# Layer norms between stages: for every second inner tile ScalarE adds the shift in a pass of its own and GpSimd makes the low half

## The chip, the cores and the metric

The kernel runs on one core of one Trainium2 chip. The metric is the device time of the program in microseconds (us). Five engines with a queue each work side by side: TensorE (PE in the profile; its weight loads are listed as PEld), VectorE (DVE), ScalarE (ACT), GpSimd (POOL) and SyncE (SP), which only starts DMAs here. An engine takes its instructions in the order in which they stand in its queue, and waits at the head of the queue for what an instruction needs.

## The reference, cut to what matters

Two layers of a diffusion backbone on 512 latent tokens and 256 context tokens, width 1024. Each layer has two modulated norms, one ahead of the token mixers and one ahead of the SwiGLU feed-forward:

```
h  = _rmsnorm(x, g_norm1) * (1.0 + sc1) + sh1      # ahead of the input projection
...
x  = x + ga1 * (o @ w_out)
h2 = _rmsnorm(x, g_norm2) * (1.0 + sc2) + sh2      # ahead of the feed-forward
x  = x + ga2 * ((silu(h2 @ w_ff1) * (h2 @ w_ff3)) @ w_ff2)
```

The context stream goes through the same formulas with its own shift and scale; the second layer needs it only in its mixers. The result is the latent stream.

## The kernel before

Activations lie transposed: features on the 128 partitions, in eight inner tiles (k = 0 to 7, `KT = 8`), tokens along the free axis. All large products are made from split numbers: a weight and an activation are each held as a high half of reduced width (`F32R`) and a low half, value minus high half, and `mm3` (L237 to L241) adds three products: high by high, high weight by low activation, low weight by high activation.

`norm_apply` (L320 to L333) makes the split activation of a norm. `parts` are stretches of tokens: 0 to 512 and 512 to 768 in the first two places below, 0 to 256 and 256 to 512 in the third. For each part and each inner tile k:

- L329, VectorE: `xn = x * gsc * pb`. `gsc` is gain times (1 + scale), a column; `pb`, in PSUM, is the inverse root mean square spread over the partitions.
- L331, ScalarE: `h[0] = xn + shift`, written at reduced width: the high half.
- L332, VectorE: `h[1] = (xn + shift) - h[0]`: the low half.

`xn` is a tile of a pool with two buffers, so a third multiplication waits until a buffer is read out. `issue_after(lows[-ahead].ins)` with `ahead = 2` also puts the multiplication of a tile behind the low half of the tile two before it, in VectorE's queue.

`norm_apply` is called four times. The first call, ahead of the first layer's mixers, works `in_place`. The other three are the places that matter here, called places 1, 2 and 3: in `dense` of layer 0 (`h2`, some 486 to 510 us), in `run` ahead of the second layer's mixers (some 1076 to 1102 us), and in `dense` of layer 1 (some 1388 to 1405 us). That makes 3 x 2 x 8 = 48 tiles.

TensorE consumes the halves at once: in `dense` for the first feed-forward tile (`f == 0`), in `proj_t` for the first two projection tiles. In both it walks k from 0 to 7 for a part, six matmuls for each k (two weights, three products), and then does the next part. `norm_finish` ends a part's statistics: a chain of tiny VectorE instructions (`rsqrt`, L249 to L255) and the spreading of the result by transposes on TensorE (`bcast`, L276). The transposes of the second part stand in TensorE's queue among or behind the matmuls of the first.

Beside this, `weights` (L222 to L235) loads a 512 KB weight tile, makes its high half on ScalarE (L231) and its low half on VectorE (L232, two inputs in SBUF). The order of each queue is worked out when the program is built, by a planner that plays the program through with its own costs and takes the ready instruction of highest priority; `issue_after` and the pools bind it.

Of the kernel before, what the change touches and what calls it, by code (L numbers as in the profile page):

```python
# [12 lines left out]
AF = mybir.ActivationFunctionType  # L13
ALU = mybir.AluOpType
# [169 lines left out]
class _Core:  # L184
# [135 lines left out]
    def norm_apply(self, x, pbs, parts, gsc, sh, h, in_place=False, ks=range(KT)):  # L320
        nc = self.nc
        lows = []
        ahead = 3 if in_place else 2
        for pb, (sl, i) in zip(pbs, parts):
            w = sl.stop - sl.start
            for k in ks:
                xn = x[:, k, sl] if in_place else self.xn.tile([P, NT], F32, name="xn")[:, :w]
                with self.tc.issue_after(lows[-ahead].ins) if len(lows) >= ahead else ExitStack():
                    nc.vector.scalar_tensor_tensor(xn, x[:, k, sl], gsc[:, k, i:i + 1], pb[:, :w],  # L329
                                                   op0=ALU.mult, op1=ALU.mult)  # L330
                nc.scalar.activation(h[0][:, k, sl], xn, AF.Identity, bias=sh[:, k, i:i + 1])  # L331
                lows.append(nc.vector.scalar_tensor_tensor(h[1][:, k, sl], xn, sh[:, k, i:i + 1], h[0][:, k, sl],  # L332
                                                           op0=ALU.add, op1=ALU.subtract))  # L333
        return lows[-1]

    def setup(self):
# [1121 lines left out]
```

## Time and profile before

| | |
|---|---|
| time of three runs, median | 1770.11 us (1770.05 to 1770.53) |
| time of the profiled execution | 1768.27 us |
| its span in the trace | 1766.5 us |
| mean granted TensorE clock | 0.981 of full |
| busy share: PE, DVE, ACT, POOL | 96%, 58%, 30%, 4% |

The span is the time from the first to the last instruction in the trace; the time of the execution is 1.77 us more. The runs' median stands 1.84 us above the profiled execution. A busy TensorE is not TensorE at its peak, since matmuls overlap. "Idle before, releaser" in a row says how long the engine did nothing just before an instruction, and what ended that.

### The profile page before, as it was taken

The numbers are of one execution on the slowest core, as the hardware profiler recorded it, in microseconds if no ns is written. First come the engines' busy times: TensorE is split into PE (matmuls) and PEld (weight loads), VectorE is DVE, ScalarE is ACT, GpSimd is POOL, SyncE is SP. The second block draws the span as 40 slices with busy tenths as digits, with TensorE's granted clock in tenths as the row PEclk, the third lists the DMA queues.
The fourth block names the chain that finished last, engine by engine and source line by source line (L and its number), as shares of the span: only waits on it lengthen the run. The fifth ranks groups of instructions, "written<-read, shape, count | busy, mean of one in ns | idle before, by whom it ended". The sixth has DMA issues, their size and how long they took to land.

```text
span 1766.5 us, 25597 instructions
## 1 busy us (share of the span) xinstructions
PE 1691.6 (96%) x10142; PEld 1373.8 (78%) x10142; DVE 1017.0 (58%) x2503; ACT 528.3 (30%) x852; POOL 67.3 (4%) x116
## 2 busy tenths in 40 slices
PE   4899899999999999999999998999999999999999
PEld 1678777676878888888888886788777888888887
DVE  7887546583387545445967537376677634333443
ACT  2422344452241212121121224225444423213221
POOL 2111000000000000000000000010000000000000
PEclk9899999999999999999999999999999999999999
DMA  9245440515134435243253332342330123223232
GB/s 365 86 149 179 144 173 26 175 53 195 60 133 135 137 128 162 89 155 125 73 163 89 103 107 94 128 126 79 115 108 25 52 92 120 96 72 119 95 90 78
DMA packets 83065, 207.25 MB, mean 117 GB/s; under 512 B 15360, under 2 KB 35968, under 8 KB 82816
## 3 DMA queue, kind: packets, MB, share of 16 engines
q1 hardware_dynamic: 54160, 160.44, 27.7%
q0 software_dynamic: 7824, 29.38, 5.0%
q10 hardware_dynamic: 20960, 15.78, 2.9%
q8 instruction: 80, 1.31, 0.3%
q14 instruction: 41, 0.34, 0.1%
HBM read 185.68 MB, written 21.99 MB: 118 GB/s over the span
## 4 chain that ended last, share of the span: by engine, by line
PE 88%; DVE 6%; DMA 2%; issue 2%; ACT 1%; SPq 0%; POOL 0%; DVEq 0%; ACTq 0%
PE psD L241 63%; PE psS L932 3%; PE psD L703 3%; PE psT L703 2%; PE psQ L979 2%; PE psQ L990 1%; PE psT L241 1%; PE psQ L1045 1%; DVE lo L232 1%; PE psT L278 1%; PE psT L376 1%; PE psT L856 1%; PE psT L265 1%; PE psS L801 1%; PE psQ L1030 1%
## 5 line engine op out<-in xcount | busy, mean ns | idle before, releaser
L241 PE MATMUL psD<-big,hi 128*128 128x512 f32 (+1 forms) x2368 | 601.5, 358 | 11.4 <-ACT big L331 7.7
L241 PEld LDWEIGHTS psD<-big,hi 128*128 128x128 f32 x2368 | 395.3, 189 | 87.7 <-ACT big L331 10.4
L231 ACT CAST hi<-raw 128x1024 fp32r<-128x1024 f32 (+1 forms) x178 | 184.3, 1039 | 753.1 <-PE psD L241 653.8
L241 PE MATMUL psD<-big,lo 128*128 128x512 f32 (+1 forms) x1184 | 365.3, 356 | 0.0
L232 DVE TENSOR_TENSOR lo<-raw,hi 128x1024 fp32r<-128x1024 f32 (+1 forms) x178 | 214.6, 1210 | 175.9 <-ACT hi L231 174.1
L241 PEld LDWEIGHTS psD<-big,lo 128*128 128x128 f32 x1184 | 201.1, 189 | 35.5 <-issue 0.4
L241 PE MATMUL psD<-gh,hi 128*128 128x512 f32 (+1 forms) x528 | 163.4, 360 | 7.5 <-DVE xb L1253 7.5
L241 PE MATMUL psD<-gl,hi 128*128 128x512 f32 (+1 forms) x528 | 165.8, 359 | 0.0
L241 PE MATMUL psD<-gh,lo 128*128 128x512 f32 (+1 forms) x528 | 165.2, 358 | 0.0
L1337 DVE TENSOR_TENSOR sg<-sg,psD 128x768 f32<-128x768 f32 (+1 forms) x44 | 36.1, 820 | 151.7 <-PE psD L241 151.7
L1253 DVE SCALAR_TENSOR_TENSOR xb<-psD,mod,xb 128x512 f32<-128x512 f32 (+1 forms) x112 | 64.6, 613 | 102.0 <-PE psD L241 101.7
L241 PEld LDWEIGHTS psD<-gh,hi 128*128 128x128 f32 x528 | 89.7, 189 | 27.0 <-DVE xb L1253 11.2
L241 PEld LDWEIGHTS psD<-gl,hi 128*128 128x128 f32 x528 | 89.7, 189 | 16.5 <-issue 0.6
L241 PEld LDWEIGHTS psD<-gh,lo 128*128 128x128 f32 x528 | 89.7, 189 | 15.8
L407 DVE CUSTOM_DVE_ANT_0 junk<-wmt,cb,pcol 128x1024 f32<-128x1024 f32 x64 | 82.1, 1283 | 29.9 <-DMA wmt<-in_wmodT 28.2
L1253 DVE SCALAR_TENSOR_TENSOR xq<-psD,mod,xq 128x512 f32<-128x512 f32 (+1 forms) x64 | 42.2, 681 | 75.0 <-PE psD L241 75.0
L241 PE MATMUL psD<-h,hi 128*128 128x512 f32 (+1 forms) x288 | 75.3, 350 | 1.5 <-DVE h L332 0.9
L932 PE MATMUL psS<-k,q 64*128 64x256 f32 (+1 forms) x432 | 71.4, 325 | 1.0 <-ACT pe L1025 0.6
L932 PEld LDWEIGHTS psS<-k,q 64*128 64x128 f32 x432 | 52.2, 185 | 19.9 <-issue 9.5
L241 PEld LDWEIGHTS psD<-h,hi 128*128 128x128 f32 x288 | 50.1, 192 | 11.2 <-issue 2.7
L241 PE MATMUL psD<-on,hi 128*128 128x256 f32 (+1 forms) x176 | 51.6, 332 | 1.2 <-ACT on L1081 1.1
L241 PE MATMUL psD<-on,lo 128*128 128x256 f32 (+1 forms) x176 | 50.2, 324 | 0.0
(404 smaller groups left out, 2321.3 us busy)
## 6 DMA issues: line engine op xcount, KB each, us to landing
raw<-in_w_ff SPq DMA_DIRECT2D x132, 512.0 KB, 3.6
wmt<-in_wmodT SPq DMA_DIRECT2D x48, 512.0 KB, 4.0
wm<-in_wmod SPq DMA_DIRECT2D x28, 512.0 KB, 6.4
raw<-in_winT SPq DMA_DIRECT2D x18, 512.0 KB, 4.2
room<-in_wmod SPq DMA_DIRECT2D x12, 512.0 KB, 11.8
nab<-in_nab SPq DMA_DIRECT2D x8, 640.0 KB, 5.2
rot<-trot POOLq DMA_DIRECT2D x8, 576.0 KB, 6.1
cf<-in_four POOLq DMA_DIRECT2D x8, 520.0 KB, 5.3
```

The source lines that it names most:

```text
L231: nc.scalar.copy(hi, raw)
L232: nc.vector.tensor_sub(lo, raw, hi)
L241: nc.tensor.matmul(o, lhsT=lhs[i], rhs=rhs[j][..., s], start=start and n == 0, stop=stop and n == 2)
L265: nc.tensor.matmul(pc[:, t], lhsT=s[:rows, t * P:(t + 1) * P], rhs=sel, start=True, stop=True)
L278: self.nc.tensor.matmul(dst, lhsT=src, rhs=self.ident, start=True, stop=True)
L376: nc.tensor.matmul(ps[32 * j:32 * j + 32], lhsT=self.cvec[:, k], rhs=ws[k // 2][:, k % 2], start=half == 0, stop=half == 1)
L407: nc.vector.tensor_tensor_reduce(junk, w, cb[:, i], 1.0, self.pcol[1][:, PC_B + f:PC_B + f + 1], op0=ALU.mult, op1=ALU.add, accum_out=mod[ ...
L703: nc.tensor.matmul(ps, lhsT=h[i][:, k, tk], rhs=w[j][:, k % per], start=k == 0 and q == 0, stop=k == KT - 1 and q == 2)
L932: self.nc.tensor.matmul(dst, lhsT=q2[i][h, qc], rhs=view(k2[j][h]), start=n == 0, stop=n == 2)
L979: nc.tensor.transpose(pp[:, k - k0], pe[:, k * P:(k + 1) * P], self.ident)
L1253: self.nc.vector.scalar_tensor_tensor(x[:, m, sl], ps[:, sl], gate[:, m, i:i + 1], x[:, m, sl], op0=ALU.mult, op1=ALU.add)
L1337: nc.vector.tensor_mul(sg, sg, pp[1])
```

## The change

Tiles with an even k, and all tiles of the in-place call, stay as they were. For odd k the shift is added by a pass of its own on ScalarE, in place in the float32 tile; a second ScalarE pass copies it to the high half; and GpSimd subtracts to make the low half. The list `lows` then holds only the low halves of even tiles, so `lows[-2]` reaches four tiles back where it reached two.

```
-                nc.scalar.activation(h[0][:, k, sl], xn, AF.Identity, bias=sh[:, k, i:i + 1])
-                lows.append(nc.vector.scalar_tensor_tensor(h[1][:, k, sl], xn, sh[:, k, i:i + 1], h[0][:, k, sl],
-                                                           op0=ALU.add, op1=ALU.subtract))
+                if in_place or k % 2 == 0:
+                    nc.scalar.activation(h[0][:, k, sl], xn, AF.Identity, bias=sh[:, k, i:i + 1])
+                    lows.append(nc.vector.scalar_tensor_tensor(h[1][:, k, sl], xn, sh[:, k, i:i + 1], h[0][:, k, sl],
+                                                               op0=ALU.add, op1=ALU.subtract))
+                else:
+                    nc.scalar.activation(xn, xn, AF.Identity, bias=sh[:, k, i:i + 1])
+                    nc.scalar.copy(h[0][:, k, sl], xn)
+                    nc.gpsimd.tensor_sub(h[1][:, k, sl], xn, h[0][:, k, sl])
```

## Rows read from the trace of the kernel before

**Rows 1.** The page, part 1: busy us (share of the span) and instructions.

```profile
PE 1691.6 (96%) x10142; PEld 1373.8 (78%) x10142; DVE 1017.0 (58%) x2503; ACT 528.3 (30%) x852; POOL 67.3 (4%) x116
```

**Rows 2.** Groups by line and shape, VectorE: busy us, mean ns, idle before.

```profile
L332 DVE SCALAR_TENSOR_TENSOR big<-xn,mod,big 128x256 fp32r<-128x256 f32 x32 | 14.3, 482 | 2.2 <-ACT big L331 2.2
L332 DVE SCALAR_TENSOR_TENSOR big<-xn,mod,big 128x512 fp32r<-128x512 f32 x16 | 11.6, 747 | 0.0
L329 DVE SCALAR_TENSOR_TENSOR xn<-xb,gsc,psQ 128x512 f32<-128x512 f32 x16 | 11.5, 742 | 0.0
...
L329 DVE SCALAR_TENSOR_TENSOR xn<-xb,gsc,psQ 128x256 f32<-128x256 f32 x16 | 6.9, 476 | 4.5 <-PE psQ L276 4.5
```

**Rows 3.** The same view, ScalarE.

```profile
L331 ACT ACTIVATE big<-xn,mod 128x256 fp32r<-128x256 f32 x32 | 14.7, 503 | 23.1 <-DVE xn L329 23.1
...
L331 ACT ACTIVATE big<-xn,mod 128x512 fp32r<-128x512 f32 x16 | 11.3, 723 | 12.2 <-DVE xn L329 12.2
```

**Rows 4.** Stretches: us, then PE, PEld, DVE, ACT, POOL busy (count), granted clock, DMA share, GB/s.

```profile
486.19:501.04 14.85, 13.52 (x58) 10.68 (x53) 12.25 (x31) 5.72 (x8) 0.00 (x0) 0.89 0.38 155
488.00:492.50 4.50, 4.50 (x16) 3.62 (x16) 4.50 (x11) 1.79 (x3) 0.00 (x0) 0.62 0.83 341
501.46:510.07 8.61, 7.46 (x48) 6.19 (x48) 6.76 (x16) 3.95 (x9) 0.00 (x0) 1.00 0.00 0
1076.43:1092.60 16.17, 14.05 (x52) 10.18 (x53) 14.71 (x33) 7.55 (x10) 0.00 (x0) 0.89 0.38 131
1388.38:1397.60 9.22, 8.15 (x54) 7.98 (x54) 8.27 (x33) 3.82 (x8) 0.00 (x0) 0.81 0.33 113
```

**Rows 5.** Timeline, place 1, VectorE: start, us, instruction, idle before.

```profile
501.46 0.87 DVE L329 SCALAR_TENSOR_TENSOR xn<-xb,gsc,psQ 128x256 f32<-128x256 f32 x2 [2.95 <-PE psQ L276]
502.51 0.89 DVE L332 SCALAR_TENSOR_TENSOR big<-xn,mod,big 128x256 fp32r<-128x256 f32 x2 [0.18 <-ACT big L331]
503.32 0.87 DVE L329 SCALAR_TENSOR_TENSOR xn<-xb,gsc,psQ 128x256 f32<-128x256 f32 x2
```

**Rows 6.** Timeline, place 1, TensorE.

```profile
498.24 0.86 PE L241 MATMUL psD<-big,hi 128*128 128x512 f32 x3
...
499.64 0.86 PE L241 MATMUL psD<-big,hi 128*128 128x512 f32 x3
...
502.54 0.91 PE L241 MATMUL psD<-big,hi 128*128 128x256 f32 x3 [1.11 <-ACT big L331]
```

**Rows 7.** Timeline, place 2, weight loads that waited for a low half.

```profile
1087.24 0.19 PEld L241 LDWEIGHTS psD<-big,hi 128*128 128x128 f32 x1 [0.42 <-DVE big L332]
...
1090.18 0.19 PEld L241 LDWEIGHTS psD<-big,hi 128*128 128x128 f32 x1 [0.31 <-DVE big L332]
```

**Rows 8.** Timeline, place 3, TensorE at the end of the first part.

```profile
1396.78 0.38 PE L276 MATMUL psQ<-cst,nr 128*128 128x128 f32 x2
```

**Rows 9.** Timeline, GpSimd: four copies, and a DMA issue behind place 2.

```profile
18.78 0.82 POOL L668 COPY ro<-sm 128x768 f32<-128x768 f32 x1 [12.06 <-DVE sm L517]
...
37.47 3.46 POOL L594 COPY bd<-bd 128x128 f32<-128x128 f32 x1
...
78.21 0.33 POOL L594 COPY bd<-bd 128x128 f32<-128x128 f32 x1 [5.15 <-DVE bg L586]
...
885.92 0.51 POOL L668 COPY ro<-sm 128x384 f32<-128x384 f32 x1 [17.72 <-DMA trot<-ro]
...
1100.19 0.54 POOL L711 DMA_DIRECT2D wglu<-in_wglu  x1 [87.61 <-DVE big L332]
```

**Rows 10.** Timeline, VectorE beside the first two of those copies.

```profile
18.38 0.20 DVE L491 SCALAR_TENSOR_TENSOR sm<-sm,sm 128x48 f32<-128x48 f32 x1
...
18.62 1.03 DVE L491 SCALAR_TENSOR_TENSOR sm<-sm,sm 128x48 f32<-128x48 f32 x2
...
40.10 0.67 DVE L632 TENSOR_TENSOR gt<-sm,bg 128x512 f32<-128x512 f32 x1
```

## Prediction

> **What bounds the kernel now.** I read the page first: TensorE is busy for 96% of the span and VectorE for 58% [rows 1]. So an engine other than TensorE matters only where TensorE waits for it. The change touches 24 of the 48 tiles of places 1, 2 and 3, so I went to the groups of L329, L331 and L332 for the price of each pass [rows 2, 3], then to the stretches and timelines of the three places to see who waits for whom.
>
> The prices: a multiplication takes 0.48 us on 256 columns and 0.74 on 512, a ScalarE pass 0.50 and 0.72, a low half 0.48 and 0.75 [rows 2, 3]. A handover costs about 0.035 us: at 501.46 a multiplication starts, 0.48 and 0.50 later would be 502.44, and the low half starts at 502.51, two handovers later [rows 5].
>
> TensorE needs 1.40 us for an inner tile of 512 columns at the full clock (498.24 to 499.64, six matmuls, 0.23 each [rows 6]), and half of that, 0.70, for 256 columns. VectorE has four passes for a pair of tiles, 2 x 0.74 + 2 x 0.75 = 2.98 us at 512 columns against TensorE's 2.80. At 256 columns its pairs come every 1.86 us (501.46 to 503.32 [rows 5]) against TensorE's 1.40. So:
>
> - Places 1 and 2, second part (256 columns): VectorE's and ScalarE's alternation sets the pace.
> - Place 2, first part (512): VectorE is busy 14.71 of 16.17 us, TensorE is busy 14.05 [rows 4] and waits 0.42 and 0.31 us for low halves [rows 7]. VectorE sets the pace here too.
> - Place 1, first part: TensorE lost time at a granted clock of 0.62 (488 to 492.5 us [rows 4]), is behind from then on, and does not wait. The low half of the last tile is wanted by the third matmul of the inner tile that starts at 499.64, so at 500.1.
> - Place 3, first part: again a mean clock of 0.81 [rows 4] and TensorE behind; it is in the last inner tile at 1396.8 [rows 8].
>
> A relief of VectorE could therefore pay in places 1 and 2. Whether this one does depends on the length of the new path.
>
> **The change, part by part.** VectorE loses 24 low halves: 8 x 0.75 + 16 x 0.48 = 13.7 us. ScalarE gains 24 passes, 8 x 0.72 + 16 x 0.50 = 13.8 us (the copy taken at the price of the pass with shift, as both read and write the same tile shape). That is covered: per pair ScalarE then has 3 x 0.50 = 1.5 or 3 x 0.72 = 2.2 us, less than any pace found below, and it is busy for 5.72 of 14.85 us and 3.95 of 8.61 us now [rows 4]. GpSimd gains 24 subtractions. The looser `issue_after` is priced at nothing, since the two buffers of `xn` bind first; without that cover it could only start multiplications earlier.
>
> The trace shows no subtraction on GpSimd. The nearest rows are copies with one input: 0.51 us for 384 columns and 0.82 for 768 [rows 9], so 0.34 us for 256 and 0.55 for 512. That is the lower bound, since a subtraction reads two inputs. The upper bound is the copy that took 3.46 us for 128 columns [rows 9], although the same shape took 0.33 at 78.21. I take twice the undisturbed copy, for two inputs: 0.65 and, rounded up from 1.10, 1.15 us. The Trainium skill, "GPSIMD Engine Reference", section 3, gives 4497 ns for a subtraction's sister, an add, on 2048 float32 columns; an estimate from that is 0.56 and 1.12 us, and by it the sum below would be about 1.3 us less.
>
> Why 3.46 us? The copy at 37.47 ends at 40.93, and VectorE's run of instructions with two inputs in SBUF ends at 40.77 [rows 9, 10]: GpSimd got through only when they were done. It works the other way as well: two instructions at 18.62 on VectorE took 1.03 us where the one at 18.38 took 0.20, beside a GpSimd copy from 18.78 to 19.60. I read this as an exclusion. The low halves (L332) and L232 have two inputs in SBUF; the multiplication (L329) reads only one there and should run free. So a low half of an even tile and the subtraction of an odd one shut each other out, and I add half a subtraction per pair: 0.33 us (256) and 0.58 us (512). The Trainium skill, "SBUF — State Buffer", section "Who interferes with whom", says just this: a VectorE instruction with two SBUF inputs contends with a GpSimd instruction that reads SBUF, and the later one blocks until the first is through; the rows agree in both directions. By that rule the sum is the one below, without it the second rival's.
>
> Now the pace. An `xn` buffer is held from the multiplication until the tile is read out. At 256 columns:
>
> - even tile: 0.48 + 0.50 + 0.48 and three handovers = 1.56 us
> - odd tile: 0.48 + 0.50 + 0.50 + 0.65 and four handovers = 2.27 us
>
> Two buffers serve two tiles per pair, so a pair takes at least (1.56 + 2.27) / 2 = 1.92 us, with the exclusion 2.25, against 1.86 now. The first odd low half comes at 0.39 + 2.24 = 2.63 us (the second multiplication of 0.87 for two starts 0.39 after the first) where it came at 502.51 + 0.89 - 501.46 = 1.94. One 256-column part thus loses 0.69 + 3 x 0.39 = 1.9 us, where TensorE has nothing else to do.
>
> At 512 columns the even tile holds 2.31 us, the odd one 0.74 + 0.72 + 0.72 + 1.15 + 0.14 = 3.47; a pair takes 2.89 us at least, 3.47 with the exclusion. The odd low halves come at 4.1 (0.7 + 3.44) and then every 3.47: the last 14.5 us after the start.
>
> - Place 1, first part: 486.19 + 14.5 = 500.7, wanted at 500.1: +0.6. Second part: +1.9.
> - Place 2, first part: the second pair waits for weights anyway; two pairs follow at 3.47 where VectorE had 2.98: +1.0. Second part: +1.9.
> - Place 3, first part: 1388.38 + 2.63 + 3 x 2.25 = 1397.8, wanted at 1396.8: +1.0. Second part: nothing; there TensorE has the matmuls of the next feed-forward tile to put in between. Without that cover it would lose up to 1.9 as well.
>
> What is given back: TensorE now stands idle 1.11 us ahead of place 1's second part, because the transposes (L276) stand behind all matmuls of the first part [rows 6]. If the planner sees TensorE wait for a last low half, it puts the transposes ahead of that, as it does at place 3 already [rows 8]. I credit half of it, 0.55, in places 1 and 2 (between 0 and 1.11).
>
> GpSimd's queue: the subtractions stand ahead of the DMA issues of `s5` (L711 and on), which already wait for the last low half until 1100.19 [rows 9]. They move with it by some 3 us and serve the stage behind the projections, so nothing. VectorE's queue: a multiplication of an odd tile that waits for GpSimd holds up the low half of the next even tile, and TensorE waits for that; this is inside the pace above.
>
> Sum: place 1 0.6 + 1.9 - 0.55 = 1.95; place 2 1.0 + 1.9 - 0.55 = 2.35; place 3 1.0; together **+5.3 us**. On the profiled execution's own 1768.27 us (its span and 1.77 us around it) that is 1773.6; on the median of the runs, 1770.11, which stands 1.84 us above it, 1775.4.
>
> The bounds: with subtractions of 0.34 and 0.55 us and no exclusion, a pair takes 1.76 us at 256 columns and TensorE's 2.80 at 512. A 256-column part loses 0.4 and wins 3 x 0.1, place 2's first part wins 2 x 0.18, and the idle 1.11 us come back twice: 0.1 - 1.11 + 0.1 - 0.36 - 1.11 = -2.4, so 1767.7. With 3.46 us for each subtraction a 256-column pair takes 3.32, the first odd low half comes at 5.4, and the three places lose 12.5, 10 and 7: 1800.
>
> **The rivals.**
>
> - *Faster.* VectorE is relieved of 13.7 us and GpSimd keeps up. Place 2's first part, where TensorE stands idle 16.17 - 14.05 = 2.1 us [rows 4], gets all of that back; with the 2 x 1.11 us, and 0.1 lost in each of the two 256-column parts, that is -4.1 or 1766.0. It decides where an odd tile's path is no slower than the pace of now: a subtraction under 0.54 us at 256 columns ((1.56 + 1.62 + 0.54) / 2 = 1.86) and under 0.97 at 512, without exclusion. For it: the lower bound. Against it: two inputs, and the exclusion of [rows 9, 10].
> - *Hidden.* My subtraction, but the exclusion costs nothing because the instructions fall between each other: pairs of 1.92 and 2.89 us. A 256-column part loses 0.69 + 3 x 0.06 = 0.87, place 2's first part wins 0.2, place 3 loses nothing, the transposes give back 0.55 to 1.11 each: +0.4 to -0.7, so 1770 to 1771.
> - *The clock falls.* With pairs of 2.25 us TensorE works 1.40 of them and waits 0.85, where it now waits 0.46 and keeps a granted clock of 1.00 [rows 4]. After the light stretch ahead of place 1 it was granted 0.62 (a mix of its two levels, 1.2 and 2.4 GHz) for 4.5 us, a loss of 0.38 x 4.5 = 1.7. If it falls in a 256-column part, a pair costs 2.80 instead of 2.25, 2.2 us more for four, and 1.7 behind it: 3.9 us in each of two places, so 1783.
>
> **How the numbers follow.** A measurement of this kernel can tell about 0.2%, 3.5 us, from no change. The forecast (+3.5 to +9 us) gets 0.50, since it rests on an exclusion that two rows show; hidden 0.27; the clock, or GpSimd held up far longer, 0.13; faster 0.10. So faster 0.10, within 0.2% 0.27, slower 0.63. The range leaves out most of the faster case and the top of the clock case: 1768 to 1786. The planner's new order moves instructions beyond these places too; that is in the range, not in the sum.
>
> **What would show it.** In the changed profile: 24 subtractions near 0.65 and 1.15 us, some stretched where they meet L332 or L232; VectorE busy down by about 13 us and ScalarE up by as much; multiplications of odd tiles that wait for POOL; pairs of about 2.25 us in the 256-column parts of places 1 and 2; TensorE's waits there put down to POOL; L276 ahead of the last matmuls of the first part. I am wrong if the subtractions take 0.5 us or less, if the pairs stay at 1.9, if the clock falls behind these waits, or if the difference arises away from the three places.

## The result and the profile after

The changed kernel takes 1779.23 us (median of 12 runs, 1774.32 to 1783.36) where the kernel before, run beside it, takes 1770.08 (12 runs): +9.2 us, a ratio of 1.0053 with a 95% interval of 1.0037 to 1.007. It is slower by 0.5%, as forecast, and inside the range; the forecast was +5.3. The profiled execution took 1774.55 us with a span of 1772.8. Behind L331 all line numbers of the changed kernel are shifted: L332 and L333 are an even tile's pass and low half, L336, L337 and L338 an odd tile's added shift, copy and subtraction; `s5`'s DMA issues are L716 and on.

The busy line of the page, against [rows 1]:

```profile
PE 1696.6 (96%) x10142; PEld 1377.0 (78%) x10142; DVE 1011.8 (57%) x2479; ACT 539.8 (30%) x876; POOL 90.0 (5%) x140
```

ScalarE gained 11.5 us, but VectorE lost only 5.2 of the forecast 13.7. The groups by line and shape say what the passes cost, against [rows 2, 3] (us in all, mean ns, idle before):

```profile
L338 POOL TENSOR_TENSOR big<-xn,big 128x256 fp32r<-128x256 f32 x16 | 11.8, 736 | 145.7 <-DMA raw<-in_w_ff 126.0 <-ACT big L337 19.7
L338 POOL TENSOR_TENSOR big<-xn,big 128x512 fp32r<-128x512 f32 x8 | 10.9, 1360 | 91.2 <-ACT big L337 91.2
L336 ACT ACTIVATE xn<-xn,mod 128x256 f32<-128x256 f32 x16 | 8.2, 509 | 12.4 <-DVE xn L329 8.9 <-POOL big L338 3.4
L333 DVE SCALAR_TENSOR_TENSOR big<-xn,mod,big 128x256 fp32r<-128x256 f32 x16 | 7.9, 496 | 6.0 <-ACT big L332 6.0
...
L333 DVE SCALAR_TENSOR_TENSOR big<-xn,mod,big 128x512 fp32r<-128x512 f32 x8 | 6.5, 809 | 2.0 <-ACT big L332 2.0
...
L337 ACT CAST big<-xn 128x256 fp32r<-128x256 f32 x16 | 6.4, 399 | 0.3
...
L337 ACT CAST big<-xn 128x512 fp32r<-128x512 f32 x8 | 4.9, 611 | 0.1
```

The subtraction takes 0.74 and 1.36 us, the copy only 0.40 and 0.61; the low halves grew by 0.01 and 0.06. Now the stretches: place 1 and the 6 us behind it, place 2 and the 8.4 us behind it (us, busy by engine, granted clock, DMA share, GB/s). A place runs here from its first multiplication to the end of its last matmul on the normed tile.

```profile
482.21:508.09 25.88, 22.57 (x107) 17.51 (x102) 17.73 (x39) 13.53 (x25) 8.11 (x8) 0.87 0.23 91
508.09:514.09 6.00, 4.51 (x17) 3.89 (x18) 4.53 (x5) 5.02 (x5) 0.00 (x0) 0.72 0.40 114
1077.12:1108.05 30.93, 22.59 (x102) 16.93 (x102) 20.06 (x41) 15.71 (x27) 12.43 (x16) 0.89 0.32 103
1108.05:1116.45 8.40, 7.00 (x21) 5.58 (x21) 2.45 (x2) 2.99 (x4) 0.00 (x0) 0.61 0.91 353
```

By the same ends the kernel before has 23.88 us in place 1 (486.19 to 510.07) and 25.21 in place 2 (1076.43 to 1101.64), and behind them granted clocks of 1.00 and 0.80. So place 1 costs 2.0 us more, place 2 costs 5.7 more, and TensorE comes out of both at a lower clock, a mix of its two levels, 1.2 and 2.4 GHz. From the first multiplication of place 3 to the end of the span it is 0.4 us more (1394.31 to 1772.80, 378.49 us, for 1388.38 to 1766.50, 378.12). The stretch between places 1 and 2 is 2.7 us longer: 1.5 of it lies right behind place 1, and 1.3 at a clock of 0.98 for 1.00 around 725 to 831 us, where the change does nothing. The stretch between places 2 and 3 is 0.5 shorter, and the one ahead of place 1, which the change does not touch, was 4.0 us shorter. Together 2.0 + 2.7 + 5.7 - 0.5 + 0.4 - 4.0 = 6.3 us, the difference of the two spans.

Where place 2's 5.7 us go is seen on the timelines of its end (start, us, idle before): GpSimd, then the ScalarE copy and the TensorE wait that answer to it.

```profile
1101.35 0.73 POOL L338 TENSOR_TENSOR big<-xn,big 128x256 fp32r<-128x256 f32 x1 [1.99 <-ACT big L337]
1102.65 0.55 POOL L716 DMA_DIRECT2D wglu<-in_wglu  x1 [0.57 <-POOL big L338]
1103.20 0.53 POOL L739 DMA_DIRECT2D rr<-tr  x1
...
1105.87 0.56 POOL L794 DMA_DIRECT2D oo<-to  x1
1106.45 0.73 POOL L338 TENSOR_TENSOR big<-xn,big 128x256 fp32r<-128x256 f32 x1
...
1102.64 0.41 ACT L337 CAST big<-xn 128x256 fp32r<-128x256 f32 x1
...
1107.23 0.39 PE L241 MATMUL psD<-big,hi 128*128 128x256 f32 x1 [3.40 <-POOL big L338]
```

The last tile's copy was done at 1103.05. Its subtraction started at 1106.45, since six DMA issues of `s5`, 0.53 to 0.77 us each, and two memsets stand ahead of it in GpSimd's queue. TensorE waited 3.40 us, more than half of what place 2 lost.

The rest of the loss is found when each place is split where TensorE begins its second part. In place 1 that is at 500.55 us, and at 502.54 in the kernel before [rows 6]. TensorE's timeline in the changed kernel, place 1:

```profile
491.80 0.43 PE L276 MATMUL psQ<-cst,nr 128*128 128x128 f32 x2
...
499.52 0.50 PE L241 MATMUL psD<-big,hi 128*128 128x512 f32 x1 [0.62 <-POOL big L338]
...
500.55 0.40 PE L241 MATMUL psD<-big,hi 128*128 128x256 f32 x2
```

The first part, of 512 columns, takes 18.34 us from the place's first multiplication (482.21 to 500.55) where it took 16.35 (486.19 to 502.54). The second part takes 7.54 us where it took 7.53. So the 2.0 us of place 1 stand in its first part alone. Place 2 is alike: its first part takes 19.98 us (1077.12 to 1097.10) for 17.68 (1076.43 to 1094.11), and its second 10.95 for 7.53, of which 3.40 are the wait for the last subtraction.

In the first part the odd tiles set the pace. Timelines of place 1, GpSimd's, ScalarE's and then VectorE's:

```profile
485.10 1.27 POOL L338 TENSOR_TENSOR big<-xn,big 128x512 fp32r<-128x512 f32 x1 [4.96 <-ACT big L337]
490.38 1.34 POOL L338 TENSOR_TENSOR big<-xn,big 128x512 fp32r<-128x512 f32 x1 [4.01 <-ACT big L337]
493.95 1.28 POOL L338 TENSOR_TENSOR big<-xn,big 128x512 fp32r<-128x512 f32 x1 [2.22 <-ACT big L337]
498.18 1.28 POOL L338 TENSOR_TENSOR big<-xn,big 128x512 fp32r<-128x512 f32 x1 [2.96 <-ACT big L337]
499.75 0.74 POOL L338 TENSOR_TENSOR big<-xn,big 128x256 fp32r<-128x256 f32 x1 [0.29 <-ACT big L337]
502.06 0.74 POOL L338 TENSOR_TENSOR big<-xn,big 128x256 fp32r<-128x256 f32 x1 [1.58 <-ACT big L337]
...
506.57 0.73 POOL L338 TENSOR_TENSOR big<-xn,big 128x256 fp32r<-128x256 f32 x1 [1.05 <-ACT big L337]
...
489.07 0.72 ACT L332 ACTIVATE big<-xn,mod 128x512 fp32r<-128x512 f32 x1
489.70 0.61 ACT L337 CAST big<-xn 128x512 fp32r<-128x512 f32 x1
...
497.10 0.49 ACT L332 ACTIVATE big<-xn,mod 128x256 fp32r<-128x256 f32 x1
...
486.90 0.75 DVE L333 SCALAR_TENSOR_TENSOR big<-xn,mod,big 128x512 fp32r<-128x512 f32 x1
487.57 0.74 DVE L329 SCALAR_TENSOR_TENSOR xn<-xb,gsc,psQ 128x512 f32<-128x512 f32 x1
...
490.50 1.25 DVE L255 SCALAR_TENSOR_TENSOR nr<-rst,nr 128x2 f32<-128x2 f32 x1
...
500.52 0.48 DVE L329 SCALAR_TENSOR_TENSOR xn<-xb,gsc,psQ 128x256 f32<-128x256 f32 x1 [0.55 <-POOL big L338]
500.92 0.48 DVE L333 SCALAR_TENSOR_TENSOR big<-xn,mod,big 128x256 fp32r<-128x256 f32 x1
501.43 0.48 DVE L329 SCALAR_TENSOR_TENSOR xn<-xb,gsc,psQ 128x256 f32<-128x256 f32 x1
```

The four subtractions of 512 columns start within 498.18 - 485.10 = 13.08 us, so a pair takes 4.36 on average, where the prediction had 3.47. The longest step shows why. The subtraction of 485.10 frees its buffer at 486.37, but the next odd tile's multiplication comes at 487.57, behind tiny instructions and an even tile's low half (486.90) in VectorE's queue; and that odd tile's copy (489.70) stands behind an even tile's pass (489.07) in ScalarE's queue. The last odd low half of the part is done at 499.46, and TensorE starts on it at 499.52.

In the second part, four subtractions of 256 columns start within 506.57 - 499.75 = 6.82 us, so a pair takes 2.27 on average, where it took 1.86 [rows 5]. That costs TensorE nothing more than before, since the tiles come earlier: the planner has put the transposes into the middle of the first part (491.80, behind all of it in the kernel before), and ScalarE makes the first high half of 256 columns at 497.10. The multiplication at 500.52 waits for the buffer that the subtraction of 499.75 holds until 500.49. The low half behind it in VectorE's queue had its input at about 500.5 but starts at 500.92, and so the next multiplication starts at 501.43.

### The profile page after: what moved, and what is told of

It is laid out like the page before. It is cut to its first block, busy times and chain, and to the rows that moved or that the text cites. A ratio compares the mean times of both kernels' runs of the same rounds, so it can differ in the third digit from the quotient of the medians.

```text
span 1772.8 us, 25645 instructions
## 1 busy us (share of the span) xinstructions
PE 1696.6 (96%) x10142; PEld 1377.0 (78%) x10142; DVE 1011.8 (57%) x2479; ACT 539.8 (30%) x876; POOL 90.0 (5%) x140
## 4 chain that ended last, share of the span: by engine, by line
PE 86%; DVE 8%; issue 2%; ACT 2%; DMA 2%; POOL 0%; SPq 0%; DVEq 0%; ACTq 0%; POOLq 0%
PE psD L241 62%; PE psS L937 4%; PE psD L708 3%; PE psT L708 2%; PE psQ L984 1%; PE psT L241 1%; PE psT L381 1%; PE psQ L995 1%; DVE lo L232 1%; PE psQ L1050 1%; PE psT L278 1%; PE psT L861 1%; PE psT L265 1%; PE psQ L1035 1%; PE psS L806 1%
## 5 line engine op out<-in xcount | busy, mean ns | idle before, releaser
L241 PE MATMUL psD<-h,lo 128*128 128x512 f32 (+1 forms) x144 | 50.4, 350 | 0.0
## 6 DMA issues: line engine op xcount, KB each, us to landing
room<-in_wmod SPq DMA_DIRECT2D x12, 512.0 KB, 11.5
```

The costliest lines, as they stand in the source:

```text
L241: nc.tensor.matmul(o, lhsT=lhs[i], rhs=rhs[j][..., s], start=start and n == 0, stop=stop and n == 2)
```

## The experiments

Three theories were on record. **Q**: the place of the last subtraction in GpSimd's queue costs place 2 its 3.4 us. **B**: in the 256-column parts the odd tile's long hold on one of two `xn` buffers sets the pace. **X**, the rival of B and the prediction's own reading: VectorE's low halves and GpSimd's subtractions shut each other out, and that sets it. Both B and X were written for the 256-column parts. All results in one table, in us; the stretch to place 3 runs from the end of place 2 to the first multiplication of place 3, the clock is the mean of the runs' granted clocks (99 runs of before, 12 of each other). The median of before is that of the 12 runs beside the changed kernel. A ratio goes by runs of before taken beside that kernel, so it is not the quotient of these medians.

| kernel | place 1 | place 2 | to place 3 | median | ratio, 95% interval | clock |
|---|---|---|---|---|---|---|
| before | 23.88 | 25.21 | 286.7 | 1770.08 | | 0.9783 |
| changed | 25.88 | 30.93 | 286.3 | 1779.23 | 1.0053 [1.0037, 1.007] | 0.9768 |
| e1_dma_behind | 25.89 | 27.73 | 286.0 | 1776.29 | 1.0037 [1.0016, 1.0058] | 0.9764 |
| e2_more_buffers | 23.70 | 28.69 | 288.7 | 1779.79 | 1.0047 [1.0026, 1.0067] | 0.9767 |
| e3_vector_subtracts | 25.00 | 25.70 | 284.2 | 1772.77 | 1.0009 [0.999, 1.0029] | 0.9781 |
| e4_before_buffers | 24.37 | 24.15 | 289.5 | 1775.86 | 1.0029 [1.0012, 1.0046] | 0.9786 |
| e6_halves | 24.25 | 29.53 | 291.8 | 1781.31 | 1.0046 [1.0024, 1.0067] | 0.9751 |
| e7_halves_dma | 24.27 | 26.14 | 284.1 | 1771.90 | 0.999 [0.9972, 1.0008] | 0.9785 |
| e8_before_halves | 24.37 | 24.28 | 293.9 | 1776.63 | 1.0017 [0.9997, 1.0038] | 0.9776 |
| e9_vector_halves | 23.09 | 23.73 | 289.8 | 1771.22 | 0.9989 [0.9968, 1.001] | 0.9791 |
| e10_vector_early | 23.08 | 23.85 | 285.2 | 1766.57 | 0.9977 [0.9952, 1.0003] | 0.9792 |
| e11_before_early | 23.05 | 24.13 | 286.7 | 1769.92 | 0.9994 [0.9974, 1.0014] | 0.9800 |
| e12_not_place2 | 25.91 | 25.14 | 288.8 | 1775.30 | 1.0032 [1.0007, 1.0057] | 0.9770 |

Place 1 by its two parts, with TensorE's granted clock in the first; each row is one profiled execution:

| kernel | first part, 512 columns | its clock | second part, 256 columns |
|---|---|---|---|
| before | 16.35 | 0.90 | 7.53 |
| changed | 18.34 | 0.81 | 7.54 |
| e12, place 1 as in the changed kernel | 18.39 | 0.91 | 7.52 |
| e8, first part as before | 17.66 | 0.81 | 6.71 |
| e11, first part as before | 16.35 | 0.90 | 6.70 |
| e2 | 16.73 | 0.80 | 6.97 |
| e3 | 16.39 | 0.79 | 8.61 |
| e7 | 18.36 | 0.91 | 5.91 |

In the changed kernel the first part takes the same time at either clock, so its length is that of the odd tiles' path. In the kernel before it depends on the clock: 16.35 us at 0.90 and 17.66 at 0.81. So the change costs the first part 2.0 us against an execution of before like the profiled one, and 0.7 against one like e8.

**e1, the queue.** In layer 1 the DMA issues are held behind the last subtraction.

```diff
-                    nc.gpsimd.tensor_sub(h[1][:, k, sl], xn, h[0][:, k, sl])
+                    self.last_sub = nc.gpsimd.tensor_sub(h[1][:, k, sl], xn, h[0][:, k, sl])
...
-            self.s5(l, oS, nq, sp, "S")
+            with tc.issue_after(self.last_sub.ins) if l == 1 else ExitStack():
+                self.s5(l, oS, nq, sp, "S")
```

> The changed kernel, with the instructions that the s5 stage of layer 1 puts into GpSimd's queue (DMA issues and memsets) held behind the last subtraction of place 2. Theory Q (the DMA issues ahead of the last subtraction made it late): the subtraction follows its ScalarE copy within 0.1 us, TensorE's wait of 3.40 us at the end of place 2 is gone, and place 2, from its first multiplication to its last matmul, takes about 27.4 us instead of 30.85 (25.21 before the change); the clock stays at full behind it, 0.7 us more. The time falls by 3.5 to 4.5 us against the changed kernel and stays about 5 us above the kernel before. Rival (the last subtraction is late by the odd tile's own path): place 2 stays at 30 us or more. Places 1 and 3 as in the changed kernel, 25.9 us and the end 374.7 us behind the first multiplication of place 3.

GpSimd's timeline at the end of place 2 in this kernel:

```profile
1111.83 0.74 POOL L338 TENSOR_TENSOR big<-xn,big 128x256 fp32r<-128x256 f32 x1 [1.99 <-ACT big L337]
1113.61 0.73 POOL L338 TENSOR_TENSOR big<-xn,big 128x256 fp32r<-128x256 f32 x1 [1.05 <-ACT big L337]
1114.80 0.55 POOL L716 DMA_DIRECT2D wglu<-in_wglu  x1 [0.45 <-PE psD L241]
```

The subtraction comes first, and place 2 falls by 3.2 us to 27.73, 2.5 above before; its second part takes 7.56 us, as before. The clock in the 8.4 us behind it is 1.00. The stage behind did not suffer from later transfers: the stretch to place 3 is not longer. Place 1 is as in the changed kernel. Q is shown in the place. The median is 2.9 us lower, less than the 3.5 to 4.5 that Q gave, and the two intervals overlap.

**e2 and e4, more buffers.** Odd tiles take a buffer of the statistics' pool, in the changed kernel (e2) and in the kernel before (e4).

```diff
-                xn = x[:, k, sl] if in_place else self.xn.tile([P, NT], F32, name="xn")[:, :w]
+                pool, tag = (self.sq, "sq") if k % 2 else (self.xn, "xn")
+                xn = x[:, k, sl] if in_place else pool.tile([P, NT], F32, name="xn", tag=tag)[:, :w]
```

> The changed kernel, with the float32 tile of odd inner tiles taken from the statistics pool (three buffers, idle by then) instead of the pool of two. Theory B (the pace of the 256-column parts is set by the buffer that the odd tile holds from its multiplication to GpSimd's subtraction): a pair falls from about 2.2 us to about 1.5 us, where ScalarE's three passes of 0.4 to 0.5 us are next, TensorE sets the pace of the 512-column parts, and place 1 takes 22.5 to 23.5 us (25.87 in the changed kernel, 23.88 before the change). Rival X (the mutual exclusion of low halves and subtractions, as the prediction priced it): it stays as it was, so a pair stays above 2.0 us and place 1 above 25 us. The late last subtraction of place 2 may stay (3.4 us), so the time ends between 3 us below and 4 us above the kernel before under B, and 6 to 10 us above under X.

> The kernel before, with the float32 tile of odd inner tiles from the statistics pool, so that the buffers alone are seen. Theory B for the kernel before: VectorE's four passes of a 256-column pair take 4 x 0.40 to 0.44 = 1.6 to 1.75 us of the 1.86, so a pair can win 0.1 to 0.25 us; place 1 falls from 23.88 to about 23 us and place 2 from 25.21 to about 24.5, and the time is 0 to 2 us lower, within 0.2%. Rival: the two buffers cost nothing before the change, and places 1 and 2 stay within 0.2 us of where they were.

In e2 place 1 comes back to 23.70 us with every subtraction still on GpSimd, where X kept it above 25. Odd tiles have buffers of their own in both parts here, and most of the gain is in the first: 16.73 us for 18.34. The exclusion still stands in e2 (a low half took 1.62 us at 489.36 beside the subtraction of 489.15), so it is the hold on one of two buffers that the change loses by, and in the 512-column part too. Place 2 keeps two waits in GpSimd's queue, 1.11 and 1.73 us. The median, 9 us above before, lies in the band that X gave: only the places speak for B. In e4 the 256-column parts of places 1 and 2, from their transposes on, take 8.20 and 8.19 us where before has 9.03 and 9.02: two buffers bound the kernel before as well. Yet place 1, expected at about 23 us, takes 24.37, since its first part ran at the lower clock, as in e8. Both medians are higher than expected, and the stretch to place 3 grew in both; two waits found with e9 stand in both traces.

**e3, the subtraction on VectorE** (`nc.vector.tensor_sub` in place of `nc.gpsimd.tensor_sub`).

> The changed kernel, with the subtraction of odd tiles on VectorE instead of GpSimd; ScalarE's extra pass stays. It parts what GpSimd costs from what the extra ScalarE pass costs. Theory B: the odd tile's path stays long by one ScalarE pass and is shorter by 0.74 - 0.48 = 0.26 us, so a 256-column pair takes about 1.95 us, place 1 some 25 us, place 2 some 26.5 us with no late last subtraction; the time is 3 to 4 us above the kernel before. Rival X: without GpSimd there is no exclusion, and a pair comes back to the 1.86 us of VectorE's four passes, place 1 to 24.0 us, and the time to within 1.5 us of the kernel before.

Without GpSimd place 2 is 0.5 us and place 1 is 1.1 us above before. Place 1 is as B said, place 2 shorter than B's 26.5; the median is 2 us above that of the runs of before beside it, between the two bands, and before within the interval. So ScalarE's added pass and the split of the low half cost 1.6 us in these places, in their second parts (8.61 and 8.63 us for 7.53), and GpSimd with its queue costs the rest.

**e6 and e7, halves.** In the 256-column parts a pair shares one 512-column buffer, so four tiles are in flight without another pool; e7 has e1's hold as well.

```diff
-                xn = x[:, k, sl] if in_place else self.xn.tile([P, NT], F32, name="xn")[:, :w]
+                if not (in_place or w <= 256 and k % 2): buf = self.xn.tile([P, NT], F32, name="xn")
+                xn = x[:, k, sl] if in_place else buf[:, 256 * (k % 2) * (w <= 256):][:, :w]
```

> The changed kernel; in the 256-column parts the two tiles of a pair take the two halves of one 512-column xn buffer, so two pairs are in flight instead of two tiles, and no other pool is touched. Theory B (an odd tile holds one of only two buffers through ScalarE's two passes and the subtraction, and that sets the pace of the 256-column parts): place 1 from its first multiplication to its last matmul falls from 25.87 us to 23.5 to 24.2, no multiplication waits for POOL there, and the median falls by 2 to 4 us to 1775 to 1777, with the GpSimd queue's wait at the end of place 2 still in it. Rival X (the two engines that take turns on the memory, or ScalarE's third pass, set the pace): place 1 stays within 0.5 us of 25.87 and the median within 1 us of 1779.

> The run before and, in layer 1, the DMA issues of the s5 stage held behind the last subtraction. Theories B and Q together (Q: the last subtraction of place 2 stands behind seven GpSimd instructions, worth 3.4 us): place 1 23.5 to 24.2 us, place 2 25.0 to 26.0 us (30.85 in the changed kernel, 25.21 before), and the median 1771 to 1773. Theory S on the clock (TensorE's clock is lower in the changed kernel, mean 0.9768 over the runs against 0.9788 before, because TensorE waits more in the places): the mean granted clock comes back to 0.978 or 0.979. Rival P (GpSimd's work itself goes with the lower clock): the clock stays at 0.976 to 0.977 and the median at 1774 to 1776.

Place 1 falls to 24.25 and 24.27 us, just above the band that B gave (23.5 to 24.2). The gain is in the second part, 5.91 us for 7.54 in e7; the first part, where no buffer was added, stays. In e6 a multiplication of the second part still waits 1.37 us for GpSimd (505.07), which B had excluded. e6's median, 1781.31, missed the bands of both theories: the wait in GpSimd's queue, 2.68 us here, was foreseen, but its stretch to place 3 grew by 5.5 us, and its clock is the lowest of all. With both edits no loss is seen any more: e7's interval is 0.9972 to 1.0008, though both its places are a little slower than before. Stretches of e7, place 1 and behind it, then place 2 and behind it:

```profile
486.23:510.50 24.27, 20.66 (x108) 16.30 (x102) 17.57 (x39) 13.33 (x25) 8.13 (x8) 0.93 0.24 99
510.50:516.50 6.00, 4.51 (x26) 3.95 (x26) 4.52 (x5) 5.03 (x5) 0.00 (x0) 1.00 0.45 105
1076.19:1102.33 26.14, 22.00 (x102) 16.87 (x102) 19.77 (x41) 15.41 (x27) 9.39 (x10) 0.87 0.25 81
1102.33:1110.73 8.40, 6.92 (x32) 5.62 (x32) 2.45 (x2) 3.08 (x4) 3.07 (x7) 1.00 0.86 275
```

The clock behind both places is 1.00, though GpSimd does the same 24 subtractions. So it is behind place 2 of e1 and place 1 of e2, while behind place 1 of e1 and e12 it is 0.72, as in the changed kernel. In these stretches P, that GpSimd's work goes with the lower clock, falls. S, that TensorE's own waits do, fits but is not shown: with the same place 2 the kernel before has 0.80 behind it and e12 1.00. The mean clock over the runs, 0.9785 for 0.9768, fits S too, but e7's own runs lie between 0.972 and 0.982.

**e8 and e9, halves in the kernel before and with the subtraction on VectorE.**

> The kernel before, with the same halves of xn buffers in the 256-column parts. Theory B: two buffers also bound the pace of the kernel before there; its 256-column parts of places 1 and 2 fall from 9.03 and 9.02 us to about 8.2, as they did with buffers of the statistics' pool (8.20 and 8.19), and the median by 1 to 3 us to 1768 to 1770, since the waits that those buffers brought elsewhere do not come. Rival X: the parts keep 9.0 us and the median 1770.7 within 1 us.

> The changed kernel with the subtractions on VectorE and the halves of xn buffers. Against the VectorE version without halves (median 1772.77, place 1 25.00 us, place 2 25.70): Theory B lets place 1 fall to 24.0 to 24.5 and the median to 1769 to 1772. Rival X: no change. For the clock: theory S expects a mean granted clock of 0.978 to 0.979, like that of e7_halves_dma; rival P expects it 0.001 to 0.002 above that of e7_halves_dma, since here GpSimd does nothing in the places.

e8's 256-column parts take 8.21 and 8.20 us, as B said, but its median is 6.5 us above that of before, where a fall was expected. e9's places are shorter than e3's by 1.9 and 2.0 us, more than expected, and its median moved by 1.5. e9's clock, 0.9791, is 0.0006 above e7's, less than P gave. In both the stretch to place 3 ate the gain. TensorE's waits in that stretch of e9 (us in all, times, longest):

```profile
PE psD L241 <- ACT on L1087: 1.7, 1, 1.7
...
PE psD L241 <- DVE lowD L1088: 1.0, 1, 1.0
```

The kernel before has neither. They stand at the head of the last output product of layer 1's mixers. The planner had moved the four transposes of the last group norm behind the whole of the product ahead of it; in before, the changed kernel and e7 they stand ahead of that product's last two column tiles. e2, e4, e6, e8 and e12 have the same two waits. e4, e8 and e11 also wait 3.2 to 3.3 us for a sigmoid of `s5`, where before waits 0.8.

**e10 and e11, the transposes put back**, on e9 and e8.

```diff
-                    self.nc.tensor.transpose(dst, src, self.ident)
+                    self.last_bc = self.nc.tensor.transpose(dst, src, self.ident)
...
-                for k in range(2):
-                    self.mm3([(ps, slice(0, n))], [t[:, j, k] for t in w], [hi[k], lo[k]], k == 0, k == 1)
+                with self.tc.issue_after(self.last_bc.ins) if halves == (0,) and j == 3 else ExitStack():
+                    for k in range(2):
+                        self.mm3([(ps, slice(0, n))], [t[:, j, k] for t in w], [hi[k], lo[k]], k == 0, k == 1)
```

> The VectorE version with halves, and one more order: the four transposes (L276) of the last group norm of layer 1's mixers stand ahead of the last column tile of the output product, as they do in the kernel before, and not behind it. Theory O (what the buffer variants lose between places 2 and 3 is this order: TensorE waits 1.7 us for the rounded copy and 1.0 us for its low half there, in every variant whose transposes stand behind): those two waits go, the stretch from the end of place 2 to the first multiplication of place 3 falls from 289.8 us to 286 to 288, and the median by 2 to 3.5 us to 1768 to 1769.5, just under the kernel before. Rival C (that stretch is the chip's scatter of the clock): the median stays within 1 us of 1771.2.

> The kernel before with halves and the same order of the four transposes. Theory O: the median falls from 1776.6 by 2 to 4 us to 1772.5 to 1774.5, with the 3.2 us wait of the s5 stage for its sigmoid still in it; the gain of the halves in the places (0.8 us in each of two) shows in the places and not in the median. Rival C: within 1 us of 1776.6.

The same two waits in e10:

```profile
PE psD L241 <- DVE lowD L1088: 0.5, 1, 0.5
...
PE psD L241 <- ACT on L1087: 0.3, 1, 0.3
```

The edit puts the transposes ahead of the last column tile, not of the last two, and the waits shrink without going. The stretch falls from 289.8 to 285.2 us in e10, a little below its band, and from 293.9 to 286.7 in e11; the two waits are 1.9 us of each fall. The clock differs as well. In e9 it was 0.95 from 1208 to 1244 us and from 1353 to 1389, in e8 0.86 from 1213 to 1250 and 0.95 from 1360 to 1397, and in e10 and e11 it is 1.00 throughout. The later of these pieces hold the two waits; in the earlier ones the edit does nothing. So the order is shown to cost 1.9 us, and for the rest rival C, the clock's scatter, is not excluded. The medians are 4.7 and 6.7 lower, more than expected, but by runs of before beside each the ratios fall from 0.9989 to 0.9977 and from 1.0017 to 0.9994, with intervals that overlap. e10 is the lowest of all, but its interval still reaches 1: at most it is about 0.5% faster than before.

**e12, place 2 left as before.** In `norm_apply`:

```diff
-                if in_place or k % 2 == 0:
+                if in_place or k % 2 == 0 or gsc is self.gsc[1][0]:
```

> The changed kernel with the norm ahead of layer 1's mixers (place 2) as in the kernel before; places 1 and 3 as changed. Theory A (the losses stand in the places and add up): place 2 comes back to 25.2 us with the 0.7 us of the clock behind it, and the median falls by 5 to 7 us to 1772 to 1774; place 1 keeps its 25.9 us. Rival R (the changed kernel is slower by its lower clock all over, wherever the subtractions are): the median falls by no more than 3 us, to 1776 or above, and the mean granted clock stays at 0.976 to 0.977.

Place 2 is back at 25.14 us and place 1 stays at 25.91: the losses stand in the places. The median, 1775.3, lies between the two theories' bands. This kernel also has the two waits of 1.7 and 1.0 us ahead of place 3, which the changed kernel does not have, and a mean clock of 0.9770, as R expected. So A is shown for the places, and R is not excluded for the clock.

## Why the prediction was right, and where its sizes were off

- *What bounds it, and the direction.* Right. Relieving VectorE is worth nothing where an odd tile's path is longer than the pace of now; the *Faster* rival needed subtractions under 0.54 and 0.97 us, and they take 0.74 and 1.28 undisturbed.
- *Place 1, +1.95.* Measured +2.0, and that the two agree is luck. The terms were +0.6 for the first part, +1.9 for the second and -0.55 back. The first part lost 2.0, with the 1.11 us ahead of the second part all given back, so 3.1 without that; the second lost nothing. The path at 512 columns was mis-sized: odd low halves come every 4.36 us and not 3.47, the last 17.25 us after the start and not 14.5, since the sum left out the wait in VectorE's and ScalarE's queues. And the planner put the transposes much further ahead than the prediction took them to go, which covered the second part's slower pace. Against an execution of before at the lower clock, as in e8, only 0.7 of the 2.0 would be left.
- *The pair of 2.25 us.* Measured 2.27, but one of its terms was another thing. The 0.33 us for the exclusion is hardly there at 256 columns: low halves average 0.50 us where they took 0.48. What fills its place is VectorE's queue: a multiplication that waits for GpSimd holds up the next even tile's low half, by some 0.4 us at 500.52. The text named this and put it "inside the pace above"; it is on top of it. With buffers alone the second part falls to 6.97 us in e2 and 5.91 in e7.
- *The exclusion.* Real where instructions are long or waiting: the 0.15 us instruction L255 took 1.25 at 490.50 beside the subtraction of 490.38. Five tiny instructions of VectorE were stretched so, and each ended 0.01 to 0.03 us behind the subtraction beside it; L249, L254 and L255 took 4.0 us more in all, a part of why VectorE's busy time fell by only 5.2 us and not 13.7. The Trainium skill, "SBUF — State Buffer", section "Who interferes with whom", has the later of two such instructions block until the first is through; the trace agrees at 490.50 (ended 491.75, the subtraction 491.72).
- *Subtractions at 0.65 and 1.15 us.* They are 14% and 11% dearer. The copy at the price of the pass with shift was too dear (0.40 for 0.50), and the two nearly cancel. The estimate from the Trainium skill, "GPSIMD Engine Reference", section 3, 0.56 and 1.12 us, was lower still: the trace shows 0.74 and 1.28.
- *Place 2, +2.35.* Measured +5.7, and without the wait of 3.40 us +2.3, again all of it in the first part, where the sum had +1.0. The step that failed is "the subtractions stand ahead of the DMA issues ... so nothing". The planner put the last one behind six issues and two memsets. That it did so because what the subtraction waits for comes late is likely, but not shown. e1 shows the price: 3.2 us of place 2.
- *Place 3, +1.0.* Measured +0.4, and not as a late low half: TensorE has no wait for one there in the changed kernel, and its clock in the 21 us from the first multiplication is 0.84 where it was 0.92. "Second part: nothing" held.
- *The clock.* In the sum at nothing, with a rival of its own at 3.9 us in each of two places. It came true in part, and the text had named it as a sign of being wrong: 0.72 for 1.00 behind place 1, worth 1.5 us, and 0.61 for 0.80 behind place 2, where the eighth matmul on a low half starts 9.18 us behind the place (1108.05 to 1117.23) and not 8.55 (1101.65 to 1110.20), 0.6 us. Over all runs the mean clock is 0.0015 lower; a fit within each kernel gives 1.3 us for 0.001, so by this estimate about 2 us of the difference of the runs' means, 1778.8 - 1771.0 = 7.8. What sets the clock in a given run stays open: e6 and e12 have low mean clocks without all of the waits.

In sum, the terms at nothing were too small by 3.4 us (the queue) and about 2 (the clock), and the three places without the queue came to 2.0 + 2.3 + 0.4 = 4.7 against the forecast 5.3. The direction and the odd tile's long hold were right; the near agreement of the places hides that the loss is in the first parts and was forecast mostly for the second.

## What to carry to other kernels

Before work is moved to a lightly loaded engine, list what else stands in its queue at that hour, DMA issues included, and ask in which order a planner will put a late instruction among them. Price the move by how long the new path holds its buffers and what queues behind the waiting instruction, not by the busy time that it takes from the old engine: here buffers shortened the 256-column parts of the kernel before by 0.8 us each, and the relief of VectorE gave nothing. Split a loss by parts before a forecast that came true is believed: a sum can be right with its terms in the wrong places. And look for side effects of a new order far away: 2.7 us of waits at a place that no edit touched stand in six of the variants.

## What the runs showed of the hardware

- A DMA issue from GpSimd's queue occupied it for 0.53 to 0.77 us, and compute behind it waited: a subtraction with its input ready at 1103.05 started at 1106.45.
- A GpSimd subtraction of 512 columns takes 1.28 us and one of 256 takes 0.74; from these two, an estimate is 0.2 us a piece and 2.1 ns a column.
- Runs of one kernel spread by 9 to 23 us, largely with the granted clock: e1's shortest run, 1771.1 us, had 0.981 and its longest, 1783.62, had 0.973. Two traces of one kernel can so differ by several us in a stretch that no edit touches.
